# Two transformer blocks on one core: gate products two ahead, VectorE alone around the norms, residual scaled beside the short convolutions, four tiles of the last gate side by side

## Chip, core and metric

The kernel runs on one core of a Trainium2 chip. Its engines work side by side, each through its own queue in program order: TensorE (PE: matmuls and transposes into PSUM banks), VectorE (DVE), ScalarE (ACT), GpSimd (POOL), and SyncE (SP), which issues the transfers. The metric is the device time of one launch in microseconds; the time of a kernel is the median of several runs.

## What is computed

A sequence of 512 positions with 1024 features goes through two blocks (f32, batch 1). The change touches the end of the first block and the second one:

```python
# end of block 1
x = x + merged @ w_out
h = rmsnorm(x, norm_ffn_g)
u = causal_dwconv(h @ w_up, conv_ffn_w)                  # 3 taps
x = x + (silu(gate_f) * up_f) @ w_down                   # d_ff 2816
x = rmsnorm(x, norm_final_g)
...
# block 2
h = rmsnorm_2(x, norm_pre)
xbc, dt_raw, z_ssd, sc_h, sc_b, sc_c, z_sc = split(h @ w_in)
xbc = silu(causal_dwconv_2(xbc, ssd_conv_w, ssd_conv_b))
y_ssd = ssd_chunked(xs, softplus(dt_raw + dt_bias), -exp(a_log), bm, cm, d_skip)
y_ssd = rmsnorm_2(y_ssd * silu(z_ssd), ssd_norm)         # in two groups of 512 features
y_sc = sc_b * causal_dwconv_2(sc_c * sc_h, sc_conv_w) * silu(z_sc)
mix = concat([y_ssd, y_sc]) @ w_out
x = x + rmsnorm_2(mix, norm_post)
return x + sigmoid(x @ w_ple_gate) * (p @ w_ple_proj)
```

## The kernel before

**Tiles and products.** Activations lie feature-major, as tiles of 128 features by 512 positions; 1024 features are 8 tiles. Each f32 operand of a product is split in a rounded part `hi` and the rest `lo = x - hi`, and a product is three matmuls for each pair of tiles: w-hi with x-hi, w-hi with x-lo, w-lo with x-hi. One output tile of a product over 1024 features is thus 24 matmuls into one PSUM bank; four banks (`mm`) serve the products, four (`pt`) the transposes and small products. `linear` makes one output tile; `linears` makes several side by side: for each feature tile the three matmuls of every output tile, then the next feature tile.

**Weights** come as 228 chunks of eight 128x128 blocks, in the order that `order()` writes down. `t_chunk` turns a chunk `raw` into `hi` on ScalarE and `lo` on VectorE or GpSimd. `Emit.idle` makes this choice, and also the one for the normalised tiles `xn` (in `normalised`) and for one addition in `t_x2`: it keeps a model clock of each engine while the program is written out, and gives the instruction to GpSimd if that would be free soon enough, unless VectorE's model clock runs far ahead.

**The order on each engine** is written out once, before the launch. The main line (`block1`, `ffn`, `block2`) asks for products; beside it small tasks (`t_...`) are spawned for evictions, norms and gates. `drive` always advances the task whose operands will be ready first by the model clocks; what has been issued stands in its engine's queue in that order.

**The places of the change.** At the FFN norm (products `out`, then the gate and up products `fg`, `fu`) and at block 2's entry (down products `fd`, then `sh`, `sc` for three tiles, the small product for `dt`, then `xbc`), the products that come first take unnormalised tiles and are scaled behind the product. `unfold` is where the main line goes over to normalised tiles `xn`. At block 2's entry `t_final` computes the two nested norms, has the eight `xn` made, then broadcasts the column `r1` over the partitions (four transposes, one copy, tile `rs1`) and scales the eight residual tiles `xr`, which are used again only in `t_x2` at the end.

In the middle of block 2, for each of eight tiles m: the gate product `zs` (its eviction is a silu), then `short_conv(m)` with the products `sh`, `sc` (from m = 3 on), `sb`, `sz`. `t_ssd(m)` is spawned behind `zs(m)`: it loads four rows, `row` and `Ce`, per pair of heads, makes decay tiles with VectorE, an exp on ScalarE and GpSimd, and runs 28 small matmuls. Two `t_ssd` are in work at most. `t_group(g)` takes the mean square of four finished tiles, broadcasts its inverse root (`rsg`), scales the four tiles and has them split. `mix` is the product over the 16 tiles of both halves: the first eight are y_ssd, the second eight the short convolutions. Then follow `pp` (the projection of p), and with `t_post` the norm of `mix` (its mean square, tile `rspost`); `t_x2` scales `mix`, adds `xr` and splits the sum, which `pg`, the last gate product, reads. The first three tiles of `pg` are made side by side.

Of the kernel before, what the change touches and what calls it, by code (L numbers as in the profile page):

```python
# [13 lines left out]
ALU = mybir.AluOpType  # L14
# [23 lines left out]
PAIR_FFN = 3  # L38
FOLD_FFN = 3
FOLD_B2 = 3  # L40
XBC = [8, 9, 0, 1, 2, 3, 4, 5, 6, 7]


# [60 lines left out]
def order():  # L104


    one = lambda keys: [[k] for k in keys]
    kq = lambda h: one([("k", h), ("q", h)])
    vg = lambda h: one([("v", h), ("ga", h)])
    o = [START] + one([("ckv", 0), ("ckv", 1)]) + [FIRST] + one([("q", 1), ("k", 2), ("q", 2)])  # L110
    for item in GDN_ORDER:
        if item[0] == "kq":
            o += kq(item[1])
        elif item[0] == "vg":
            o += vg(item[1])
        elif item[0] == "low":
            pass
        elif item[0] == "wv":
            o += one([("wv", kt, h) for kt in range(2) for h in range(4 * item[1], 4 * item[1] + 4)])
        elif item[0] in ("bra", "brb", "ya"):  # L120
            o.append([item])
        else:
            h = item[1]
            o += one(qr_of(h) + [("kn", h), ("qn", h)])
    o += [[("yb", 0), ("yb", 1)]] + one([("yb", m) for m in range(2, 8)])
    o += one([("out", m) for m in range(8)])
    pair = lambda f: [("fg", f), ("fu", f)]
    for f in range(12):
        o += [pair(f)] if f < PAIR_FFN else one(pair(f))
    o += one([("fd", 0, m) for m in range(8)])  # L130
    o += one([x for f in range(12, 22) for x in pair(f)])
    o += one([("fd", 1, m) for m in range(8)])
    xbc = [("xbc", m) for m in XBC]
    o += [[("sh", m), ("sc", m)] for m in range(FOLD_B2)] + [["dt2"]] + one(xbc)
    for m in range(8):
        o += one([("zs", m)] + ([("sh", m), ("sc", m)] if m >= FOLD_B2 else []) + [("sb", m), ("sz", m)])
    o += one([("mix", m) for m in range(8)])
    o += one([("pp", m) for m in range(8)])
    o += [[("pg", 0), ("pg", 1), ("pg", 2)]] + one([("pg", m) for m in range(3, 8)])
    return o  # L140


# [252 lines left out]
class Emit:  # L395
# [5 lines left out]
    def __init__(self, ctx, tc, a, out):  # L401
        self.tc, self.a, self.out = tc, a, out
        self.nc = self.tl = Timeline(tc.nc)
        E = ctx.enter_context
        self.const = E(tc.tile_pool(name="const", bufs=1))
        self.wp = E(tc.tile_pool(name="wp", bufs=1))
        self.gp = E(tc.tile_pool(name="gp", bufs=1))
        self.sm = E(tc.tile_pool(name="sm", bufs=1))
        self.ps = E(tc.tile_pool(name="ps", bufs=1, space=PSUM))
        self.dr = E(tc.tile_pool(name="dr", bufs=1, space=DRAM))  # L410
        self.n = 0
        self.nmm = 0
        self.mms = []
        self.held = None
        self.specs = weight_specs()
        self.order = order()
        self.opos = 0
        self.bpos = 0
        self.blocks = {}
        self.his = {}  # L420
        self.nchunk = a["wstream"].shape[0]
        self.loaded = 0
        self.tasks = []
        self.waiting = {}
        self.nspawn = 0
        self.flags = set()
        self.live = []
        self.hold = 1 << 30
        self.using = None

    def idle(self, pool, dve, bias=0):

        now = self.tl.clk["PE"]
        t = lambda e: max(self.tl.clk[e], now)
        if t("DVE") - now > BACKLOG:
            return self.nc.vector
        return self.nc.gpsimd if t("POOL") + pool <= t("DVE") + dve + bias else self.nc.vector
# [918 lines left out]
    def block1(self):  # L1356
        nc = self.nc
# [82 lines left out]
        ps = yield from self.linears(START, self.xh)  # L1440
# [3 lines left out]
        for m in range(2):  # L1444
            ps = yield from self.linear(("ckv", m), self.xh)
            self.spawn(self.t_rows(raws["ckv"], m, ps, None, "lr"))
        yield from self.unfold()
        ps = yield from self.linears(FIRST, self.xh)
# [4 lines left out]
        ps = yield from self.linear(("q", 1), self.xh)  # L1453
# [3 lines left out]
        for item in GDN_ORDER:  # L1457
# [12 lines left out]
            elif item[0] in ("bra", "brb"):  # L1470
                ps = yield from self.linear(item, self.xh)
# [4 lines left out]
            else:  # L1476
# [6 lines left out]
                ps = yield from self.linear(item, oa)  # L1483
# [18 lines left out]
        for ms in [(0, 1)] + [(m,) for m in range(2, 8)]:  # L1502
# [3 lines left out]
            ps = yield from self.linears([("yb", m) for m in ms], ob)  # L1506
# [13 lines left out]
        for m in range(8):  # L1520
            x = self.g(name="xr")
            nc.sync.dma_start(x, self.a["xT"][m])
            ps = yield from self.linear(("out", m), mg)
            self.spawn(t_out(m, x, ps))

    def unfold(self):

        self.hold = self.bpos
        yield lambda: hasattr(self, "xn")
        self.hold = 1 << 30  # L1530
        self.xh = self.xn
        self.fold = None
        del self.xn


    def ffn(self):
        nc = self.nc
        hs = [None] * MFF
        self.fold = True

        def t_gate(d, f, ps, fold):
            d["g"] = yield from self.conv(ps, fold, "conv_ffn_w", f, 3, "fg")
            nc.scalar.activation(d["g"], d["g"], AF.Silu)

        def t_up(d, f, ps, fold):
            up = yield from self.conv(ps, fold, "conv_ffn_w", MFF + f, 3, "fu")
            yield lambda: "g" in d
            yield [d["g"]]
            nc.gpsimd.tensor_tensor(up, d["g"], up, ALU.mult)
            hs[f] = yield from self.split(up)  # L1550

        def pair(f):
            d = {}
            keys = ("fg", f), ("fu", f)
            if f < PAIR_FFN:
                pg, pu = yield from self.linears(keys, self.xh)
                self.spawn(t_gate(d, f, pg, self.fold))
            else:
                pg = yield from self.linear(keys[0], self.xh)
                self.spawn(t_gate(d, f, pg, self.fold))  # L1560
                pu = yield from self.linear(keys[1], self.xh)
            self.spawn(t_up(d, f, pu, self.fold))

        def t_down(half, m, ps):
            yield [ps]
            nc.vector.tensor_tensor(self.xr[m], self.xr[m], ps, ALU.add)
            if half:
                yield from self.final_tile(m)

        def down(half):  # L1570
            for m in range(8):
                ps = yield from self.linear(("fd", half, m), hs[11 * half:11 * half + 11] if not half else hs2)
                self.spawn(t_down(half, m, ps))

        for f in range(12):
            if f == FOLD_FFN:
                yield from self.unfold()
            yield from pair(f)
        yield lambda: hs[10] is not None
        yield from down(0)  # L1580
        for f in range(12, 22):
            yield from pair(f)
        yield lambda: hs[21] is not None
        hs2 = hs[11:]
        self.xh = [None] * 8
        del self.rs
        self.spawn(self.t_final())
        yield from down(1)
        del hs, hs2

# [6 lines left out]
    def t_final(self):  # L1597
        nc = self.nc
# [9 lines left out]
        r1 = yield from self.meanrs(self.x1, D, "fn1")  # L1608
# [10 lines left out]
        nc.gpsimd.tensor_tensor(self.rs2, self.rs, self.rs, ALU.mult)  # L1619
        self.xn = [None] * 8  # L1620
        yield from self.normalised(self.x1, self.gg, self.rs, True, self.xn)
        r1b = yield from self.bcast(r1, "rs1")
        self.xr = self.x1
        for m in range(8):
            nc.vector.scalar_tensor_tensor(self.xr[m], self.xr[m], self.par("norm_final_g", m), r1b,
                                           ALU.mult, ALU.mult)
            yield [self.xr[m]]


    def dts(self):  # L1630

# [258 lines left out]
    def block2(self):  # L1890
        nc = self.nc
# [16 lines left out]
        self.spawn(self.t_group(0))  # L1908
        self.spawn(self.t_group(1))
        zd = {}  # L1910
        for m in range(8):
            ps = yield from self.linear(("zs", m), self.xh)
            self.spawn(self.t_rows(zd, m, ps, AF.Silu, "zs"))
            self.spawn(self.t_ssd(m, zd), "ssd")
            yield from self.short_conv(m)
        mix = [None] * 8
        self.spawn(self.t_post(mix))
        for m in range(8):
            ps = yield from self.linear(("mix", m), self.ym)
            self.spawn(self.t_rows(mix, m, ps, None, "mix"))  # L1920
        ph, pp = [None] * 2, {}
# [4 lines left out]
        for m in range(8):  # L1926
            ps = yield from self.linear(("pp", m), ph)
            self.spawn(self.t_rows(pp, m, ps, None, "pp"))
        x2 = [None] * 8
# [20 lines left out]

        for m in range(8):
            self.spawn(t_x2(m))
        ps = yield from self.linears([("pg", m) for m in range(3)], x2)
        for m in range(3):
            self.spawn(t_fin(m, ps[m]))
        for m in range(3, 7):
            ps = yield from self.linear(("pg", m), x2)
            self.spawn(t_fin(m, ps))

# [69 lines left out]
```

## Time and profile before

| | |
|---|---|
| median of 3 runs | 1471.09 us (1470.6 to 1472.59) |
| profiled execution, its own time | 1473.28 us |
| its span, first to last instruction | 1471.5 us |
| mean granted TensorE clock | 0.993 of full |
| busy: PE, DVE, ACT, POOL | 1444.7, 854.4, 657.8, 542.6 us |

The profile is of one execution. An engine's busy time is the sum of its instructions' durations; matmuls overlap one another, so that a row of a matmul is longer than the time to the next one's start. The granted clock is the share of full speed that the chip's throttle let TensorE have. In a row of the timeline, the bracket gives how long the engine had been idle before the instruction, and which engine's instruction, on which tile, ended that wait.

### The profile page before, as it was taken

Reading aid. Unit: us, or ns where it says so; the run is one execution under the profiler, and the core shown is the slowest. Engines: PE = TensorE matmul, PEld = TensorE weight load, DVE = VectorE, ACT = ScalarE, POOL = GpSimd, SP = SyncE. Lnnn points to the kernel's source line nnn. Section 1 sums busy time; section 2 is a strip of 40 time slices with the busy share of each in tenths; the row PEclk is TensorE's granted clock in tenths of the full one; section 3 lists DMA queues with packets and bytes.
Section 4 is the critical chain, followed back from the end, with each engine's and each line's share of the span. In section 5 each row is a group of like instructions: output and inputs, shape, how many; then the busy total and the mean of one; then the engine's idle time right before and its main releaser. Section 6 shows DMA issues by size and latency. Waiting matters only on the chain.

```text
span 1471.5 us, 18957 instructions
## 1 busy us (share of the span) xinstructions
PE 1444.7 (98%) x7084; PEld 1188.1 (81%) x7084; DVE 854.4 (58%) x1701; ACT 657.8 (45%) x1120; POOL 542.6 (37%) x333
## 2 busy tenths in 40 slices
PE   9999999999999999999999999999999999999998
PEld 6788788778878888888888888888787778878877
DVE  7988879687755554367441244446975564360073
ACT  4664335234555663445442244444544544442342
POOL 0333500520334314434554455444024434534421
PEclk9999999999999999999999999999999999999999
DMA  5434313331122224423333223332233433422322
GB/s 190 134 116 143 108 58 85 117 99 32 58 86 74 85 79 129 150 86 101 100 100 101 90 96 100 100 91 88 67 115 113 117 108 102 135 87 86 100 87 100
DMA packets 56891, 147.62 MB, mean 100 GB/s; under 512 B 15008, under 2 KB 15584, under 8 KB 56800
## 3 DMA queue, kind: packets, MB, share of 16 engines
q1 hardware_dynamic: 56800, 146.42, 32.5%
q8 instruction: 55, 0.90, 0.2%
q14 instruction: 36, 0.29, 0.1%
HBM read 139.48 MB, written 5.34 MB: 98 GB/s over the span
## 4 chain that ended last, share of the span: by engine, by line
PE 79%; DVE 13%; POOL 3%; issue 2%; ACT 1%; DMA 1%; SPq 1%; DVEq 0%; POOLq 0%; ACTq 0%
PE mm L244 71%; PE pt L244 8%; DVE lo L244 3%; POOL st L244 1%; POOL sx L244 1%; DVE st L244 1%; DVE sx L244 1%; DVE mix L244 1%; SPq L244 1%; ACT hi L244 0%; DVE Y L244 0%; DVE rq_u L244 0%; DVE qrs L244 0%; DMA x<-xT 0%; DVE v L244 0%
## 5 line engine op out<-in xcount | busy, mean ns | idle before, releaser
L244 PE MATMUL mm<-hi,hi 128*128 128x512 f32 (+2 forms) x1872 | 741.6, 396 | 3.4 <-ACT hi L244 3.4
L244 PE MATMUL mm<-lo,hi 128*128 128x512 f32 (+2 forms) x1872 | 727.0, 388 | 4.5 <-DVE lo L244 4.5
L244 PE MATMUL mm<-hi,lo 128*128 128x512 f32 (+2 forms) x1872 | 726.7, 389 | 2.5 <-DVE lo L244 2.5
L244 POOL TENSOR_TENSOR lo<-raw,hi 128x1024 fp32r<-128x1024 f32 x152 | 365.2, 2403 | 536.4 <-ACT hi L244 509.0
L244 PEld LDWEIGHTS mm<-hi,lo 128*128 128x128 f32 x1872 | 352.6, 188 | 77.9 <-DVE lo L244 4.2
L244 PEld LDWEIGHTS mm<-hi,hi 128*128 128x128 f32 x1872 | 352.9, 188 | 73.8 <-ACT hi L244 4.3
L244 PEld LDWEIGHTS mm<-lo,hi 128*128 128x128 f32 x1872 | 353.3, 189 | 71.4 <-DVE lo L244 5.6
L244 ACT ACTIVATE hi<-raw 128x1024 fp32r<-128x1024 f32 (+1 forms) x230 | 242.5, 1054 | 229.1 <-PE mm L244 164.4
L244 DVE TENSOR_TENSOR lo<-raw,hi 128x1024 fp32r<-128x1024 f32 (+1 forms) x78 | 97.4, 1249 | 3.5 <-ACT hi L244 3.5
L244 DVE TENSOR_TENSOR sq<-sq,sq 128x512 f32<-128x512 f32 x43 | 32.6, 771 | 93.8 <-ACT sq L244 93.6
L244 DVE TENSOR_TENSOR xr<-xr,mm 128x512 f32<-128x512 f32 x24 | 16.5, 687 | 97.5 <-PE mm L244 97.5
L244 DVE TENSOR_TENSOR lo<-fu,hi 128x512 fp32r<-128x512 f32 x22 | 44.5, 2023 | 42.0 <-ACT hi L244 42.0
L244 DVE SCALAR_TENSOR_TENSOR fu<-mm,params,fu 128x510 f32<-128x510 f32 (+1 forms) x38 | 28.5, 749 | 61.6 <-ACT fu L244 60.9
L244 ACT ACT_TABLE_LOAD x39 | 50.0, 1283 | 13.2 <-DVE k L244 6.0
L244 POOL TENSOR_TENSOR q<-q,row 128x512 f32<-128x512 f32 x8 | 10.6, 1319 | 96.6 <-PE pt L244 86.8
L244 POOL TENSOR_TENSOR fu<-fg,fu 128x512 f32<-128x512 f32 x22 | 30.0, 1365 | 42.8 <-DVE fu L244 42.8
L244 DVE TENSOR_TENSOR lo<-scz,hi 128x512 fp32r<-128x512 f32 x8 | 15.8, 1969 | 32.7 <-ACT hi L244 32.7
L244 POOL TENSOR_TENSOR st<-sl,sx 64x247 f32<-64x247 f32 (+15 forms) x31 | 20.8, 672 | 34.3 <-DVE sx L244 25.0
L244 ACT ACTIVATE fg<-fg 128x512 f32<-128x512 f32 x22 | 13.9, 631 | 40.2 <-DVE fg L244 40.2
L244 DVE SCALAR_TENSOR_TENSOR fg<-mm,params,fg 128x510 f32<-128x510 f32 (+1 forms) x38 | 28.2, 743 | 6.2 <-ACT fg L244 5.5
L244 POOL TENSOR_TENSOR xdd<-xd,dd 128x512 f32<-128x512 f32 x8 | 9.4, 1176 | 60.3 <-DVE xd L244 60.2
L244 DVE TENSOR_TENSOR lo<-pt,hi 128x512 fp32r<-128x512 f32 (+3 forms) x32 | 15.6, 487 | 25.9 <-ACT hi L244 25.7
(312 smaller groups left out, 1552.7 us busy)
## 6 DMA issues: line engine op xcount, KB each, us to landing
raw<-wstream SPq DMA_DIRECT2D x228, 512.0 KB, 3.6
row<-grow_d SPq DMA_DIRECT2D x16, 256.0 KB, 4.4
row<-crow_d SPq DMA_DIRECT2D x16, 256.0 KB, 4.7
x<-xT SPq DMA_DIRECT2D x8, 256.0 KB, 5.9
sbd<-gate SPq DMA_DIRECT2D x8, 256.0 KB, 2.1
sb<-sbd SPq DMA_DIRECT2D x8, 256.0 KB, 3.9
xr<-xT SPq DMA_DIRECT2D x8, 256.0 KB, 3.8
Ce<-crow_d SPq DMA_DIRECT2D x16, 128.0 KB, 5.0
```

What stands on the lines that cost most here:

```text
L244: return f(*args, **kw)
```

## The change

Four things. `PAIR_PG`: the first four tiles of `pg` are made side by side, where three were. `ZS = 2`: the gate products `zs` run two tiles ahead of the short convolutions, and `t_ssd` with them. `norming`: while this flag is set, `idle` gives everything to VectorE; it is set from the seventh `out` product to the FFN's `unfold`, from the seventh `fd` product of the second half to block 2's `unfold`, and from the seventh `mix` product to the end. Residual: the broadcast of `r1` and the eight scalings of `xr` move from `t_final` to a task `t_residual(m)` behind each `short_conv(m)`. The number of instructions on PE, ACT and SP stays what it was; 21 go from POOL (338 to 317) to VectorE (1547 to 1568).

```diff
+PAIR_PG = 4
+ZS = 2
 # order(): the weights' order follows the products
+    o += one([("zs", m) for m in range(ZS)])
     for m in range(8):
-        o += one([("zs", m)] + ([("sh", m), ("sc", m)] if m >= FOLD_B2 else []) + [("sb", m), ("sz", m)])
+        o += one(([("sh", m), ("sc", m)] if m >= FOLD_B2 else []) + [("sb", m), ("sz", m)])
+        if m + ZS < 8:
+            o += one([("zs", m + ZS)])
...
-    o += [[("pg", 0), ("pg", 1), ("pg", 2)]] + one([("pg", m) for m in range(3, 8)])
+    o += [[("pg", m) for m in range(PAIR_PG)]] + one([("pg", m) for m in range(PAIR_PG, 8)])
...
     def idle(self, pool, dve, bias=0):
+        if self.norming:
+            return self.nc.vector
...
         for m in range(8):                                   # block 1, "out"
...
+            self.norming = m >= 6
             ps = yield from self.linear(("out", m), mg)
...
     def unfold(self):
...
+        self.norming = False
...
             for m in range(8):                               # down(half)
+                self.norming = half == 1 and m >= 6
                 ps = yield from self.linear(("fd", half, m), ...)
...
     def t_final(self):
...
-        r1b = yield from self.bcast(r1, "rs1")
         self.xr = self.x1
-        for m in range(8):
-            nc.vector.scalar_tensor_tensor(self.xr[m], self.xr[m], self.par("norm_final_g", m), r1b,
-                                           ALU.mult, ALU.mult)
-            yield [self.xr[m]]
+        self.r1 = r1
+
+    def t_residual(self, m):
+        if m == 0:
+            self.r1b = yield from self.bcast(self.r1, "rs1")
+        yield lambda: hasattr(self, "r1b")
+        yield [self.r1b]
+        self.nc.vector.scalar_tensor_tensor(self.xr[m], self.xr[m], self.par("norm_final_g", m), self.r1b,
+                                            ALU.mult, ALU.mult)
...
-        for m in range(8):                                   # block 2
+        def zs(m):
             ps = yield from self.linear(("zs", m), self.xh)
             self.spawn(self.t_rows(zd, m, ps, AF.Silu, "zs"))
             self.spawn(self.t_ssd(m, zd), "ssd")
+        for m in range(ZS):
+            yield from zs(m)
+        for m in range(8):
             yield from self.short_conv(m)
+            self.spawn(self.t_residual(m))
+            if m + ZS < 8:
+                yield from zs(m + ZS)
...
         for m in range(8):
+            self.norming = m >= 6
             ps = yield from self.linear(("mix", m), self.ym)
```

**Block 2's entry, VectorE.** The rows around the eviction `dtz` of the small product for `dt`: `dtw` is its weights, `sh` and `ysc` belong to the short convolutions, `lo<-raw,hi` is half of a weight chunk. Before:

```order
L244 SCALAR_TENSOR_TENSOR lo_9311<-xn_9273,gg_8547,hi_9302 128x512
L244 SCALAR_TENSOR_TENSOR xr_6104<-xr_6104,params,rs_9299 128x512
L244 TENSOR_TENSOR lo_9322<-raw_9308,hi_9317 128x1024
L244 SCALAR_TENSOR_TENSOR xr_6143<-xr_6143,params,rs_9299 128x512
L244 SCALAR_TENSOR_TENSOR xr_6183<-xr_6183,params,rs_9299 128x512
L244 SCALAR_TENSOR_TENSOR xr_6224<-xr_6224,params,rs_9299 128x512
L244 SCALAR_TENSOR_TENSOR ysc_9352<-sh_9282,params,ysc_9352 128x510
L244 SCALAR_TENSOR_TENSOR ysc_9352<-sh_9282,params,ysc_9352 128x511
L244 SCALAR_TENSOR_TENSOR xr_6265<-xr_6265,params,rs_9299 128x512
L244 COPY dtz_9348<-pt_9331 32x512
```

The same place in the changed kernel:

```order
L249 SCALAR_TENSOR_TENSOR lo_9273<-xn_9252,gg_8547,hi_9268 128x512
L249 TENSOR_TENSOR lo_9280<-raw_9266,hi_9275 128x1024
L249 COPY dtw_9290<-hi_9177 128x4x16
L249 COPY dtw_9290<-lo_9189 128x4x16
L249 COPY dtw_9291<-hi_9177 128x4x16
L249 COPY dtw_9291<-lo_9189 128x4x16
L249 TENSOR_TENSOR sh_9288<-mm_9199,sh_9288 128x512
L249 SCALAR_TENSOR_TENSOR ysc_9325<-sh_9288,params,ysc_9325 128x510
L249 SCALAR_TENSOR_TENSOR ysc_9325<-sh_9288,params,ysc_9325 128x511
L249 COPY dtz_9323<-pt_9306 32x512
```

The five scalings of `xr` that stood between the last `lo` of an `xn` and `dtz` are gone from there, and three more behind it; further up, between the norm's last step and `dtz`, VectorE has all eight `xn`, of which POOL had three, and four weight halves as before; a fifth weight half stands inside the norm's own steps.

**Ahead of `mix`, TensorE.** `pt<-sqc,rs` are the four transposes that broadcast the second group's inverse root; the tile `mm_11469` is `mix`'s first output. Before:

```order
L244 MATMUL mm_11420<-lo_9300,hi_11329 128x512
L244 MATMUL mm_11420<-hi_9277,lo_11331 128x512
L244 MATMUL pt_11458<-sqc,rs_11395 128x128 x4
L244 MATMUL mm_11420<-hi_9302,hi_11329 128x512
L244 MATMUL mm_11420<-lo_9311,hi_11329 128x512
L244 MATMUL mm_11420<-hi_9302,lo_11331 128x512
L244 MATMUL mm_11469<-hi_10574,hi_11329 128x512
```

In the changed kernel the same transposes stand here:

```order
L249 MATMUL mm_11279<-hi_9256,hi_11188 128x512
L249 MATMUL mm_11279<-lo_9261,hi_11188 128x512
L249 MATMUL mm_11279<-hi_9256,lo_11190 128x512
L249 MATMUL pt_11317<-sqc,rs_11254 128x128 x4
L249 MATMUL mm_11279<-hi_9268,hi_11188 128x512
L249 MATMUL mm_11279<-lo_9273,hi_11188 128x512
```

Three matmuls stood between these transposes and `mix`'s first matmul; now there are 99: the end of one product tile and the four products of the last short convolution.

**Ahead of `pg`, VectorE.** From the last step of the inverse root of `mix` to the first tiles that `pg` reads. Before:

```order
L244 SCALAR_TENSOR_TENSOR rs_12071<-rq_u_12073,rs_12071 128x4
L244 SCALAR_TENSOR_TENSOR mix_11556<-mix_11556,params,rspost_12133 128x512
L244 SCALAR_TENSOR_TENSOR mix_11621<-mix_11621,params,rspost_12133 128x512
L244 SCALAR_TENSOR_TENSOR mix_11687<-mix_11687,params,rspost_12133 128x512
L244 TENSOR_TENSOR mix_11556<-mix_11556,xr_6104 128x512
L244 TENSOR_TENSOR mix_11621<-mix_11621,xr_6143 128x512
L244 TENSOR_TENSOR mix_11687<-mix_11687,xr_6183 128x512
L244 TENSOR_TENSOR lo_12170<-mix_11556,hi_12166 128x512
```

In the changed kernel:

```order
L249 SCALAR_TENSOR_TENSOR rs_12071<-rq_u_12073,rs_12071 128x4
L249 TENSOR_TENSOR lo_12140<-raw_12124,hi_12126 128x1024
L249 SCALAR_TENSOR_TENSOR mix_11556<-mix_11556,params,rspost_12120 128x512
L249 TENSOR_TENSOR mix_11556<-mix_11556,xr_6104 128x512
L249 SCALAR_TENSOR_TENSOR mix_11621<-mix_11621,params,rspost_12120 128x512
L249 SCALAR_TENSOR_TENSOR mix_11687<-mix_11687,params,rspost_12120 128x512
L249 TENSOR_TENSOR lo_12167<-mix_11556,hi_12160 128x512
L249 SCALAR_TENSOR_TENSOR mix_11753<-mix_11753,params,rspost_12120 128x512
L249 TENSOR_TENSOR mix_11621<-mix_11621,xr_6143 128x512
L249 TENSOR_TENSOR mix_11687<-mix_11687,xr_6183 128x512
L249 TENSOR_TENSOR mix_11753<-mix_11753,xr_6224 128x512
L249 TENSOR_TENSOR lo_12191<-mix_11621,hi_12184 128x512
```

A weight half now stands ahead of the first `mix`, the first sum follows its scaling at once, and a fourth tile is made before the second tile's `lo`. On ScalarE the `hi` of that same weight chunk stands directly ahead of the copy of `rspost`.

## Rows read from the trace of the kernel before

**Rows 1.** The page, part 1: busy time, share, instructions.

```profile
PE 1444.7 (98%) x7084; PEld 1188.1 (81%) x7084; DVE 854.4 (58%) x1701; ACT 657.8 (45%) x1120; POOL 542.6 (37%) x333
```

**Rows 2.** Groups of instructions: count | busy us, mean ns of one | idle before.

```profile
L244 PE MATMUL mm<-hi,lo 128*128 128x512 f32 (+2 forms) x1872 | 726.7, 389 | 2.5 <-DVE lo L244 2.5
L244 POOL TENSOR_TENSOR lo<-raw,hi 128x1024 fp32r<-128x1024 f32 x152 | 365.2, 2403 | 536.4 <-ACT hi L244 509.0
L244 DVE TENSOR_TENSOR lo<-raw,hi 128x1024 fp32r<-128x1024 f32 (+1 forms) x78 | 97.4, 1249 | 3.5 <-ACT hi L244 3.5
```

**Rows 3.** Windows: length, busy PE PEld DVE ACT POOL, granted clock, DMA share, GB/s.

```profile
650.00:675.00 25.00, 25.00 (x112) 20.72 (x111) 24.40 (x30) 14.53 (x21) 4.32 (x3) 1.00 0.26 82
1025.00:1050.00 25.00, 22.62 (x97) 16.69 (x96) 24.79 (x37) 11.28 (x16) 3.59 (x3) 0.93 0.21 66
```

**Rows 4.** TensorE at block 2's entry: timeline, and the window behind the wait.

```profile
1044.22 0.43 PE L244 MATMUL pt<-sqc,dtz 32*128 32x32 f32 x4 [2.27 <-DVE dtz L244]
...
1045.38:1048.80 3.42, 3.42 (x10) 2.67 (x9) 3.35 (x6) 1.63 (x2) 0.00 (x0) 0.50 0.00 0
```

**Rows 5.** POOL's and VectorE's timelines at block 2's entry.

```profile
1014.83 1.29 POOL L244 TENSOR_TENSOR xn<-xr,rs 128x512 f32<-128x512 f32 x1
...
1016.91 1.01 DVE L244 SCALAR_TENSOR_TENSOR lo<-xn,gg,hi 128x512 fp32r<-128x512 f32 x1 [6.71 <-ACT hi L244]
...
1039.41 2.07 DVE L244 SCALAR_TENSOR_TENSOR xr<-xr,params,rs 128x512 f32<-128x512 f32 x3
```

**Rows 6.** Timeline ahead of mix (PE, VectorE), and the window behind the wait.

```profile
1303.51 0.60 PE L244 MATMUL pt<-sqc,sq 128*128 128x128 f32 x4
...
1304.88 0.17 DVE L244 TENSOR_SCALAR ms_a<-cs 128x4 f32<-128x4 f32 x1
...
1312.84 0.60 PE L244 MATMUL pt<-sqc,rs 128*128 128x128 f32 x4
...
1320.71 0.50 PE L244 MATMUL mm<-lo,hi 128*128 128x512 f32 x1 [3.59 <-DVE lo L244]
...
1322.07:1325.06 2.99, 2.99 (x9) 2.34 (x8) 0.99 (x2) 0.00 (x0) 0.00 (x0) 0.50 0.31 114
```

**Rows 7.** Timeline ahead of pg: VectorE, POOL, ScalarE, TensorE.

```profile
1410.21 2.41 POOL L244 TENSOR_TENSOR lo<-raw,hi 128x1024 fp32r<-128x1024 f32 x1 [3.73 <-ACT hi L244]
...
1410.43 2.20 DVE L244 SCALAR_TENSOR_TENSOR ms_a<-cs,ms_a 128x4 f32<-128x4 f32 x1
...
1414.65 0.16 DVE L244 SCALAR_TENSOR_TENSOR rs<-rq_u,rs 128x4 f32<-128x4 f32 x1
1415.01 1.06 ACT L244 ACTIVATE hi<-raw 128x1024 fp32r<-128x1024 f32 x1
...
1417.06 3.36 DVE L244 SCALAR_TENSOR_TENSOR mix<-mix,params,rspost 128x512 f32<-128x512 f32 x3 [2.25 <-ACT rspost L244]
...
1421.06 1.83 ACT L244 ACTIVATE hi<-mix 128x512 fp32r<-128x512 f32 x3 [1.40 <-DVE mix L244]
...
1421.74 0.49 PE L244 MATMUL mm<-hi,hi 128*128 128x512 f32 x1 [2.70 <-ACT hi L244]
1422.89 0.50 PE L244 MATMUL mm<-lo,hi 128*128 128x512 f32 x1 [0.65 <-DVE lo L244]
...
1429.62 0.50 PE L244 MATMUL mm<-lo,hi 128*128 128x512 f32 x1 [0.28 <-DVE lo L244]
```

**Rows 8.** Timeline at the first SSD products (PE, VectorE, ScalarE), and ScalarE before the second.

```profile
1115.41 2.76 DVE L244 TENSOR_SCALAR row<-row,cmp 128x128 f32<-128x128 f32 x8
...
1117.42 0.64 ACT L244 ACTIVATE row<-row 128x512 f32<-128x512 f32 x1 [5.60 <-DVE row L244]
...
1121.65 0.66 PE L244 MATMUL pt<-row,xd 128*64 128x128 f32 x8
...
1132.79 1.28 ACT L244 ACT_TABLE_LOAD   x1
1134.08 1.20 ACT L244 ACTIVATE row<-row 128x512 f32<-128x512 f32 x2
```

More of the change, by code (lines that the diff above doesn't have):

```diff
@@ L1532, in unfold @@
         self.fold = None
+        self.norming = False
         del self.xn
@@ L1621, in t_final @@
         yield from self.normalised(self.x1, self.gg, self.rs, True, self.xn)
-        r1b = yield from self.bcast(r1, "rs1")
         self.xr = self.x1
-        for m in range(8):
-            nc.vector.scalar_tensor_tensor(self.xr[m], self.xr[m], self.par("norm_final_g", m), r1b,
-                                           ALU.mult, ALU.mult)
-            yield [self.xr[m]]
+        self.r1 = r1
[6 more added lines that the diff above has]
+                                            ALU.mult, ALU.mult)
+        if m == 7:
+            del self.r1b
     def dts(self):
@@ L1952, in block2 @@
             self.spawn(t_x2(m))
-        ps = yield from self.linears([("pg", m) for m in range(3)], x2)
-        for m in range(3):
+        ps = yield from self.linears([("pg", m) for m in range(PAIR_PG)], x2)
+        for m in range(PAIR_PG):
             self.spawn(t_fin(m, ps[m]))
-        for m in range(3, 7):
+        for m in range(PAIR_PG, 7):
             ps = yield from self.linear(("pg", m), x2)
```

## Prediction

> **What bounds the kernel.** I read the page first: TensorE is busy 98% of the span, every other engine under 60% [rows 1]. So only time in which TensorE waits, or runs slower than it can, is to be had. Then I went through the windows of 25 us: nearly all read like the first of [rows 3], TensorE 25.00 of 25 us with 112 matmuls, one for each 0.22 to 0.23 us; I use 0.23. From the FFN norm on, where the change begins, three places are different, and there I read the timelines.
>
> *A, block 2's entry* [rows 4]. The transposes of `dtz` come after 2.27 us of idle, released by VectorE's `dtz`. A matmul row lasts 0.39 us [rows 2] but the next one starts after 0.23, so an idle time of t costs t + 0.16: here 2.43. Soon behind it the granted clock reads 0.50, the 1.2 GHz level, for 3.42 us, in which every matmul takes twice its time: 1.7 lost. A costs 4.1 us. Why `dtz` is late is in the VectorE rows: 24.79 of 25 us busy [rows 3], with eight scalings of `xr` in its queue, five of them directly ahead of `dtz`, 2.07 us for three [rows 5]. Earlier VectorE had been idle for 6.71 us until 1016.91, because the first `xn` was made on POOL at 1014.83, behind a weight half of 2.40 us.
>
> *B, ahead of `mix`* [rows 6]. Group 1's mean square is transposed at 1303.51, its inverse root broadcast at 1312.84; then the scalings, `hi`, `lo`, and TensorE goes on at 1320.71 after 3.59 us of idle: 3.75 lost, and half of the 2.99 us at clock 0.50 behind it, 1.5. B costs 5.25.
>
> *C, ahead of `pg`* [rows 7]. Idle 2.70, 0.65 and 0.28: with 0.16 each 2.86, 0.81 and 0.44, together 4.1. The clock does not fall here.
>
> The ceiling is A + B + C = 13.45 us. Time on VectorE or POOL elsewhere is worth nothing.
>
> **The change part by part.**
>
> *Residual later, and `norming` at block 2's entry (A).* Off VectorE's queue ahead of `dtz` go five `xr`, 0.69 each [rows 5], 3.45 us; on it come three `xn` that POOL made. I have no row of an `xn` on VectorE here; a tile of this size is 0.69 in these rows, so 2.07. More is won at the start: the first `xn` no longer waits for POOL. VectorE was through with the norm at 1010.2 (1016.91 - 6.71); four transposes (0.60, as in [rows 6]) and a copy (0.61, as a `hi` in [rows 7]) put the broadcast at 1011.4, and the first `xn` follows it, not at 1014.83. From there to the last `dtw` the changed order has 21 tile operations, four weight halves and the four small casts: 21 x 0.69 + 4 x 1.2 + 0.4 = 19.7, so 1031.1. TensorE has 93 matmuls between the norm's transposes and the small product, 21.4 us, and wants `dtw` at about 1031.9. Just in time. Behind the small product only six matmuls, 1.4 us, stand ahead of `dtz`'s transposes (fifteen before), with an eviction of 0.7 to be done in them; and the norm's own transposes come six matmuls earlier, while the inserted weight half keeps the root from coming earlier: up to 0.5 of wait. I keep 0.6 us for such small waits. With the long wait the slow stretch should go; the clock is low in these rows only behind the longest idle times (2.27 and 3.59), not behind C's 2.70, so that is not certain. Gain 3.5. Bounds: 1.8 (the wait goes, but the clock falls all the same and the small waits stay) to 4.1.
>
> The moved scalings then stand one behind each short convolution, 0.69 of VectorE per tile of three to five products, 5.5 us each. The broadcast's four transposes move with them and cost TensorE what they did, 0.60 like those of [rows 6]. Nothing.
>
> *`zs` two ahead (B).* Three matmuls stood between group 1's broadcast and `mix`; now 99, 22.8 us. Its mean square's transposes stand 39 matmuls ahead of the broadcast's, 9.0 us, where the rows have 9.3 without a wait. From the broadcast to TensorE's restart took 1320.71 - 1312.84 = 7.9 us, of which twelve `mix` matmuls were covered before as well. All of the wait goes, with 15 us to spare, whatever the added `xr` scaling and weight half there cost (0.7 and 1.2). Gain 5.25; bounds 3.75 (the clock falls at `mix` for another reason) to 5.25.
>
> The price stands at the first SSD products [rows 8]. Tiles 0 and 1 are now prepared together: sixteen VectorE operations where eight take 2.76 us, and ScalarE's order becomes exp, table load, silu of `zs1`, table load, exp, weight `hi`, exp, exp. From the first exp at 1117.42: 0.64, 1.28, 0.60, 1.28, 0.64 gives 1121.9, one product with `cb` on VectorE (0.69) gives 1122.6. TensorE has nine matmuls more to do before it (39, not 30), so it comes at 1121.65 + 2.1 = 1123.7. The second tile: 1121.9 + 1.06 + two exps + 0.69 = 1124.9, needed 28 small matmuls later (0.66 for eight), at about 1126.0. Margin 1.1 in both; cost 0, and at worst rival 2.
>
> *`norming` and four tiles (C).* `ms_a` took 2.20 us, to 1412.63, as long as POOL's weight half beside it (to 1412.62), where 0.17 is usual [rows 6, 7]. POOL does none of these now: 2.0 us won, but one weight half (1.14 to 1.25 [rows 2]) stands inside the norm's steps: the root is ready at about 1413.8 instead of 1414.81. The scalings of `mix` no longer take 3.36 for three, but 0.69 each. Against that: on ScalarE a weight `hi` now stands ahead of the copy of `rspost`, and it can't be sooner than its transfer, 1415.01 to 1416.07; then the `lo` of that chunk, 1.2, ahead of the first scaling, which starts at 1417.25. Scaling, sum, `hi` (0.69, 0.69, 0.61): 1419.2. TensorE comes free at 1421.74 - 2.86 = 1418.9 as before: wait 0.3 to 0.4. The first tile's `lo` comes behind two more scalings, at 1420.4 to 1420.7, where 1419.5 is wanted: 0.9 to 1.2. With four tiles side by side a step is 12 matmuls, 2.7 us, not 2.0, against 2.0 to 2.6 us of VectorE (scaling, sum, `lo`, and a weight half at each second step); I keep 0.3 for the second step. Left 1.65, gain 4.1 - 1.65 = 2.45. Bounds 1.0 (waits as long as the upper values, and two more) and 3.8.
>
> *FFN norm.* No wait of TensorE now, though VectorE is busy 24.40 of 25 us [rows 3]. It gets four weight halves and two `xn`, some 6 us, and loses what POOL's halves stretched. I take nothing; if its cover is gone, that is 0 to 3 us.
>
> Sum: 3.5 + 5.25 + 2.45 = 11.2 from the profiled execution's own 1473.28: 1462.1. That execution is 2.19 us above the median of the runs, so 1471.09 - 11.2 = **1459.9**.
>
> **The rivals.**
>
> 1. *VectorE stays the bound at A.* For it: the queue is full (24.79 of 25), and `idle` now adds to it. The Trainium skill, page "Perfetto Trace Analysis", section "Optimizing Scalar/DVE Operations", says that some work of a saturated VectorE may well be given to GpSimd, which is the reverse of this edit; it adds that the two share a port, so it might not help. Against: VectorE stood idle 6.71 us while POOL made the first `xn` [rows 5], and an instruction of 0.17 took 2.20 beside a POOL one [rows 7]. If the three `xn` and the inserted weight half (2.07 + 1.25) cost as much as the five scalings saved (3.45), A stays whole: 1459.9 + 3.5 = 1463.4.
>
> 2. *A new wait at the first SSD products.* For it: margins of 1.1 us on a chain of eight ScalarE steps. If each of the two loads held ScalarE for twice its 1.28, the tiles would come 1.5 us late (2.56 less 1.1): with the 0.16, and perhaps a slow stretch of 1.7, 1461.5 to 1463.2. Against: an exp starts at 1134.08 right behind a load of 1.28 at 1132.79 [rows 8], so I go by 1.28. The Trainium skill's page "ScalarE: Activation LUTs", section "What ACT_TABLE_LOAD costs", gives 2.66 us in all per switch, of which 1.28 is the load; by that the two switches would take 2.76 more than I count, and the time would be 1461.7 to 1463.4. This trace doesn't show the rest of it.
>
> 3. *C gives nothing back*, because TensorE now waits for the `hi` and `lo` of the weight chunk ahead of `rspost` instead: 1459.9 + 2.45 = 1462.35.
>
> 4. *Slower.* `t_ssd` prepares in the shade of the products, eight rounds; if the new place of `zs` left each round short, each would wait. Against: the loop is the same behind each `zs`, and TensorE has no wait in these rounds now. It decides from 11.2 / 8 = 1.4 us per round; at 2 us with no clock loss it gives 1475.9.
>
> **How the numbers follow.** The forecast's chain 0.64 (own range 1457.6 to 1462); rival 1 0.10, rival 2 0.12, rival 3 0.07; slower 0.04; no effect, since waits only change places, 0.03. Two runs of one kernel tell 0.2% apart, 2.9 us. All of the first four are faster than 1468.2; for misses of several at once I move 0.04 to the other two: faster 0.89, same 0.06, slower 0.05. The range goes from 1457 (the ceiling 1471.09 - 13.45 = 1457.6, rounded down for the runs' own spread) to 1465 (rival 1 with a further 1.5).
>
> **What would show it.** Right: `dtz` released TensorE without idle, VectorE's first `xn` near 1011.4 in place of POOL's; no idle and clock 1.00 around the first `mix`; `ms_a` 0.17 at C and two or three idle times under 1.2 us each at the first `pg`. Wrong: idle over 1 us ahead of the first two SSD tiles, at the FFN norm or at `dt2`, or a clock of 0.50 anywhere from the FFN on; a POOL weight half still beside the norms. If the time stays over 1465, a wait has opened that stands in no row here.

## The result and the profile after

The changed kernel took 1464.43 us in the median of 8 runs (1461.31 to 1468.91), the kernel before 1473.01 us in 8 runs, three of them those given above: ratio 0.9935, 95% interval 0.9924 to 0.9946, that is 9.6 us less (8.0 to 11.2; the two medians alone differ by 8.6). Forecast were 11.2 us less. The profiled execution took 1465.11 us, with a span of 1463.3 us against 1471.5.

The windows of 25 us are read as in [rows 3]. TensorE's idle time is the length of the window, 25.00, less the number behind it; the granted clock stands behind POOL.

```profile
1000.00:1025.00 25.00, 24.91 (x117) 20.48 (x116) 21.86 (x52) 11.14 (x15) 3.22 (x3) 1.00 0.25 68
1025.00:1050.00 25.00, 23.87 (x109) 18.06 (x108) 21.00 (x45) 10.86 (x15) 5.69 (x3) 1.00 0.26 82
1100.00:1125.00 25.00, 24.34 (x148) 18.82 (x146) 14.35 (x28) 11.73 (x14) 10.54 (x9) 1.00 0.43 106
1300.00:1325.00 25.00, 25.00 (x112) 20.71 (x111) 8.32 (x9) 6.30 (x9) 11.22 (x5) 1.00 0.31 98
1400.00:1425.00 25.00, 23.83 (x107) 18.80 (x106) 19.08 (x39) 13.68 (x22) 0.00 (x0) 1.00 0.29 85
```

Ahead of `mix` (around 1310) nothing is lost, and the clock is 1.00 in all five. What is left are four waits, all that the view of waits lists for TensorE from 560 us to the end; here they stand in the timeline:

```profile
1034.43 0.39 PE L249 MATMUL pt<-hi,dtw 128*32 128x512 f32 x1 [1.13 <-DVE dtw L249]
...
1123.27 0.44 PE L249 MATMUL pt<-row,xd 128*64 128x128 f32 x4 [0.66 <-DVE row L249]
...
1413.72 0.49 PE L249 MATMUL mm<-hi,hi 128*128 128x512 f32 x1 [0.39 <-ACT hi L249]
1414.98 0.50 PE L249 MATMUL mm<-lo,hi 128*128 128x512 f32 x1 [0.77 <-DVE lo L249]
```

To these come 0.25 us lost ahead of the norm's transposes at 1011.58 and 0.17 at 1418.05, where the starts lie 0.48 and 0.40 apart and not 0.23. With 0.16 for each idle time over 0.3, as in the prediction, the losses are: entry 0.25 + 1.29, ahead of `pg` 0.55 + 0.93 + 0.17. The first SSD products are small matmuls with shorter distances, and their wait of 0.66 costs 1.1: from the first of them to the next product they take 5.93 us, and 4.85 in a kernel further down in which the same 56 matmuls don't wait (`Ce` of the second tile on VectorE). Together 4.3, where the prediction counted 13.45 before: 9.2 won, inside the interval of the runs.

The span fell by only 8.2. In this execution the granted clock was 0.50, the 1.2 GHz level, from 417.76 on, in a part of the program that the change does not touch: TensorE's matmuls are 0.1 us later than in the profile before ahead of it, and 1.7 behind it, the same up to 990. From there to the end 9.9 us are won, of which the count above finds 9.2. The window before, then after:

```profile
417.76:421.17 3.41, 3.41 (x18) 2.84 (x17) 2.48 (x7) 1.20 (x4) 0.00 (x0) 1.00 0.45 144
...
417.76:421.17 3.41, 3.41 (x11) 2.83 (x11) 1.89 (x5) 0.67 (x2) 0.00 (x0) 0.50 0.44 144
```

At the entry VectorE makes the first `xn`, as forecast, but it is stretched. VectorE and POOL, first piece of the stage:

```profile
1012.86 2.14 DVE L249 TENSOR_TENSOR xn<-xr,rs 128x512 f32<-128x512 f32 x2 [1.42 <-ACT rs L249]
1014.92 2.31 DVE L249 TENSOR_TENSOR lo<-raw,hi 128x1024 fp32r<-128x1024 f32 x1
...
1025.38 1.78 DVE L249 SCALAR_TENSOR_TENSOR lo<-xn,gg,hi 128x512 fp32r<-128x512 f32 x1
...
1033.99 0.19 DVE L249 CAST dtw<-hi 128x64 fp32r<-128x64 f32 x1
...
1012.90 1.55 POOL L249 TENSOR_TENSOR rs<-rs 128x512 f32<-128x512 f32 x1 [30.88 <-ACT rs L249]
1014.52 1.62 POOL L249 TENSOR_TENSOR sh<-sh,rs 128x512 f32<-128x512 f32 x1
1024.95 1.67 POOL L249 TENSOR_TENSOR sh<-sh,rs 128x512 f32<-128x512 f32 x1 [8.80 <-DVE sh L249]
```

`norming` takes from POOL only what `idle` decides. Two kinds of instruction that the code gives to POOL by name are left there: `rs2` and the products of `sh` with it. Each of the three shown lies over a VectorE instruction that is 0.85 to 1.1 us longer than usual. From the start of the first `xn` to the end of the last `dtw` 21.6 us pass, where the prediction had 19.7.

At the first SSD products, VectorE, ScalarE and POOL:

```profile
1113.90 6.42 DVE L249 TENSOR_SCALAR row<-row,cmp 128x128 f32<-128x128 f32 x16
...
1118.00 0.64 ACT L249 ACTIVATE row<-row 128x512 f32<-128x512 f32 x1 [7.70 <-DVE row L249]
1118.65 1.28 ACT L249 ACT_TABLE_LOAD   x1
1119.95 0.60 ACT L249 ACTIVATE zs<-mm 128x512 f32<-128x512 f32 x1
1120.56 1.28 ACT L249 ACT_TABLE_LOAD   x1
1121.86 0.63 ACT L249 ACTIVATE row<-row 128x512 f32<-128x512 f32 x1
...
1112.68 5.01 POOL L249 TENSOR_TENSOR Ce<-Ce,xbc 64x512 f32<-64x512 f32 x4
```

The ScalarE chain from the first exp to the second is what the prediction laid out, load for load (3.86 us against 3.80). But it begins 4.1 us behind the first row operation; before, it was 2.0 [rows 8]. The view of the tile `row` before, with the shortest, median and longest of the eight operations in ns:

```profile
L244 DVE TENSOR_SCALAR row<-row,cmp x8: 273/274/1383, 1115.4 to 1117.9; 128x128 f32<-128x128 f32 x8
```

In the changed kernel three of the sixteen are that long (last section).

### The profile page after: what moved, and what is told of

It reads as the page before. It is cut to its first block, busy times and chain, and to the rows that moved or that the text cites. A ratio compares the mean times of both kernels' runs of the same rounds, so it can differ in the third digit from the quotient of the medians.

```text
span 1463.3 us, 18957 instructions
## 1 busy us (share of the span) xinstructions
PE 1443.4 (99%) x7084; PEld 1187.8 (81%) x7084; DVE 867.9 (59%) x1722; ACT 656.2 (45%) x1120; POOL 497.5 (34%) x312
## 4 chain that ended last, share of the span: by engine, by line
PE 81%; DVE 11%; POOL 3%; issue 2%; ACT 1%; DMA 1%; SPq 1%; DVEq 0%; POOLq 0%; ACTq 0%
PE mm L249 72%; PE pt L249 8%; DVE lo L249 2%; POOL st L249 1%; POOL sx L249 1%; DVE st L249 1%; SPq L249 1%; DVE row L249 1%; DVE sx L249 1%; ACT hi L249 0%; DVE Y L249 0%; DVE qrs L249 0%; DMA sl<-ldram 0%; DVE v L249 0%; DMA x<-xT 0%
## 5 line engine op out<-in xcount | busy, mean ns | idle before, releaser
L249 POOL TENSOR_TENSOR lo<-raw,hi 128x1024 fp32r<-128x1024 f32 x136 | 327.6, 2409 | 462.2 <-ACT hi L249 399.6
L249 DVE TENSOR_TENSOR lo<-raw,hi 128x1024 fp32r<-128x1024 f32 (+1 forms) x94 | 117.1, 1245 | 27.9 <-ACT hi L249 27.9
L249 DVE SCALAR_TENSOR_TENSOR xbc<-mm,params,xbc 128x509 f32<-128x509 f32 (+2 forms) x30 | 22.5, 749 | 9.5 <-ACT xbc L249 8.8
```

The source lines that it names most:

```text
L249: return f(*args, **kw)
```

## Experiments

Ratios are to the kernel before, run beside each kernel; the changed kernel has 0.9935. Losses of TensorE are read from the profiles as above, the changed kernel's being 4.3 us.

**The gate products back in their place.**

```diff
-        for m in range(ZS):
-            yield from zs(m)
         for m in range(8):
+            yield from zs(m)
             yield from self.short_conv(m)
             self.spawn(self.t_residual(m))
-            if m + ZS < 8:
-                yield from zs(m + ZS)
```

(with the weights' order to match.) Expected:

> The changed kernel with the gate products in their old place again (zs(m), then short_conv(m)); the other three parts stay. My account: the order ahead of mix is the old one, so TensorE waits 3.5 us or more there again and the slow stretch of 1.5 may come back (4 to 5.3 us lost at mix), while the 0.7 us at the first SSD products goes: 3.5 to 4.5 us slower than the changed kernel, ratio to the kernel before about 0.996 to 0.997. Rival: the wait at mix went because VectorE and POOL are freer, whatever the order: no idle time at mix, ratio 0.993.

Measured: ratio 0.9969 (0.9954 to 0.9983), 5.0 us above the changed kernel. TensorE's timeline, the window behind the wait, and the first SSD products:

```profile
1320.92 0.80 PE L246 MATMUL mm<-lo,hi 128*128 128x512 f32 x1 [3.59 <-DVE lo L246]
...
1320.92:1324.00 3.08, 3.08 (x8) 2.48 (x9) 2.36 (x4) 0.00 (x0) 0.00 (x0) 0.53 0.64 176
...
1121.39 0.66 PE L246 MATMUL pt<-row,xd 128*64 128x128 f32 x8
```

The wait of [rows 6] is back to the hundredth, and the slow stretch with it; the wait at the first SSD products is gone, all eight run through. B's gain, and that wait, come with the new place of `zs` and go with it.

**Without `norming`.**

```diff
     def idle(self, pool, dve, bias=0):
-        if self.norming:
-            return self.nc.vector
```

> The changed kernel with the flag that gives everything to VectorE taken out; order of products, residual and four tiles stay. My account: ahead of pg the step ms_a is stretched to about 2 us again beside a POOL weight half and the wait is 3 to 4 us again, not 1.75; at block 2's entry the first xn comes from POOL about 3 us later, so dtw or dtz is waited for by 2 us or more. In all 2.5 to 4 us slower than the changed kernel, ratio 0.995 to 0.996. Rival: VectorE alone is what costs at the entry (the wait of 1.3 us for dtw), so that the entry gets faster without it and the ratio stays at 0.993 to 0.994.

Measured: ratio 0.9966 (0.995 to 0.9981), 4.6 us above the changed kernel. Timeline of POOL, VectorE and TensorE ahead of `pg`, a window behind it, and TensorE's two waits at the entry:

```profile
1406.54 2.40 POOL L249 TENSOR_TENSOR lo<-raw,hi 128x1024 fp32r<-128x1024 f32 x1 [3.72 <-ACT hi L249]
...
1406.77 2.19 DVE L249 SCALAR_TENSOR_TENSOR ms_a<-cs,ms_a 128x4 f32<-128x4 f32 x1
...
1418.08 0.51 PE L249 MATMUL mm<-hi,hi 128*128 128x512 f32 x1 [2.70 <-ACT hi L249]
1419.22 0.50 PE L249 MATMUL mm<-lo,hi 128*128 128x512 f32 x1 [0.64 <-DVE lo L249]
...
1420.02:1423.43 3.41, 3.41 (x10) 2.63 (x9) 3.41 (x6) 1.49 (x2) 0.00 (x0) 0.50 0.00 0
...
1038.65 0.50 PE L249 MATMUL mm<-lo,hi 128*128 128x512 f32 x1 [1.16 <-DVE lo L249]
...
1045.13 0.24 PE L249 MATMUL pt<-sqc,dtz 32*128 32x32 f32 x1 [0.65 <-DVE dtz L249]
```

`ms_a` is long again and C's waits are those of [rows 7], 2.70 and 0.64; this time a slow stretch follows, 3.41 us at 0.50, which costs 1.7 and takes the whole above the 2.5 to 4 us expected. At the entry 1.32 + 0.81 are lost, against 1.54 with the flag. So at the entry the flag is worth 0.6 us only.

**The residual back at the entry.**

```diff
+        r1b = yield from self.bcast(r1, "rs1")
         self.xr = self.x1
-        self.r1 = r1
+        for m in range(8):
+            nc.vector.scalar_tensor_tensor(self.xr[m], self.xr[m], self.par("norm_final_g", m), r1b,
+                                           ALU.mult, ALU.mult)
+            yield [self.xr[m]]
...
-            self.spawn(self.t_residual(m))
```

> The changed kernel with the eight scalings of xr back at block 2's entry. My account: they stand in VectorE's queue between the last xn and dtz, 0.69 each, five to eight of them: the wait for dtz comes back with 2 to 4 us, perhaps with a slow stretch of 1.7; 2 to 5 us slower than the changed kernel, ratio 0.995 to 0.997. Rival: the earlier first xn alone made the room, and the scalings fall behind dtz: ratio 0.993 to 0.994.

Measured: ratio 0.9949 (0.9932 to 0.9966), 2.1 us above the changed kernel, but the intervals overlap: the runs alone don't tell the two apart. The profile has 1.5 more lost. VectorE and TensorE:

```profile
1039.09 3.39 DVE L249 SCALAR_TENSOR_TENSOR xr<-xr,params,rs 128x512 f32<-128x512 f32 x5
1042.40 0.67 DVE L249 COPY dtz<-pt 32x512 f32<-32x512 f32 x1
...
1043.13 0.43 PE L249 MATMUL pt<-sqc,dtz 32*128 32x32 f32 x4 [0.90 <-DVE dtz L249]
```

Five scalings stand ahead of `dtz` again, but the wait is 0.90, not 2.27: `dtz` starts 31.0 us behind the norm's transposes (1042.40 - 1011.42), before it was 32.5 (1043.50 - 1011.00). That for `dtw` is 0.62, not 1.13; a wait of 0.79 for `gg` follows at 1052.03. No slow stretch. Of A's 4.1 us, 2.1 are left with the moved residual alone (the kernel without `norming`), 3.0 with the flag alone (this one) and 1.54 with both: the residual is the larger part.

**Three tiles of `pg` side by side** (`PAIR_PG = 3`).

> The changed kernel with three tiles of pg side by side instead of four. My account: the waits before the first two matmuls of pg stay (0.55 and 1.0 us); a step is 9 matmuls (2.0 us) where VectorE needs 2.0 to 2.6 us for a tile, so there are one to three more waits of 0.2 to 0.6 us: 0.3 to 1.2 us slower than the changed kernel, ratio 0.9937 to 0.9945. Rival: the fourth tile only delays the second tile's lo: with three the waits are shorter, ratio 0.993.

Measured: ratio 0.9945 (0.9927 to 0.9963), 1.5 us above the changed kernel, which the runs alone would not tell from none; the profile has 1.35 more lost. TensorE's timeline:

```profile
1414.51 0.51 PE L249 MATMUL mm<-hi,hi 128*128 128x512 f32 x1 [0.38 <-ACT hi L249]
1415.78 0.50 PE L249 MATMUL mm<-lo,hi 128*128 128x512 f32 x1 [0.76 <-DVE lo L249]
...
1418.85 0.50 PE L249 MATMUL mm<-lo,hi 128*128 128x512 f32 x1 [0.65 <-DVE lo L249]
```

The first two waits are unchanged; the second step, which 9 matmuls don't cover, now waits 0.65, and two later ones cost 0.2 and 0.4. In the profile the fourth tile is worth slightly more than I expected.

The next three kernels were measured in one execution each. Executions of one kernel lie up to 7.6 us apart (the changed one's 1461.31 to 1468.91), so their times decide nothing, and what is read is the waits.

**Two `Ce` of the second tile on VectorE**, to take half of POOL's work from beside the row operations.

```diff
-            yield [Cs[e]]
-            nc.gpsimd.tensor_tensor(Cs[e][r], Cs[e][r], self.C[r], ALU.mult)
+            if m != 1:
+                yield [Cs[e]]
+                nc.gpsimd.tensor_tensor(Cs[e][r], Cs[e][r], self.C[r], ALU.mult)
+        if m == 1:
+            for e in range(2):
+                yield Es + [Cs[e]]
+                nc.vector.tensor_tensor(Cs[e][r], Cs[e][r], self.C[r], ALU.mult)
```

> The changed kernel, with the two Ce products of the second tile's pair of heads (t_ssd(1)) on VectorE, behind its products with cb, instead of on POOL. My account: the wait of 0.7 us at the first SSD products comes from POOL: four Ce instead of two stand beside VectorE's row operations, and three of these take 1.3 us instead of 0.28. With two Ce on POOL one or two row operations are long, the first exp comes 1 to 2 us earlier (now 4.1 us behind the first row operation), and the wait of 0.93 from start to start falls to under 0.35. Rival: the two table loads on ScalarE set the time of the second exp: the row operations get shorter, but the wait stays at 0.6 to 0.9.

Measured in one execution: 1461.89 us (its mean granted clock was 0.998, the changed kernel's profile has 0.994). VectorE and ScalarE, and TensorE's first SSD products:

```profile
1111.48 4.32 DVE L249 TENSOR_SCALAR row<-row,cmp 128x128 f32<-128x128 f32 x16
...
1113.48 0.63 ACT L249 ACTIVATE row<-row 128x512 f32<-128x512 f32 x1 [5.60 <-DVE row L249]
...
1119.76 0.66 PE L249 MATMUL pt<-row,xd 128*64 128x128 f32 x8
```

Sixteen row operations take 4.32 us instead of 6.42, one of them being long and not three; the first exp comes 2.0 us behind the first of them; the eight products run through without a wait. Both table loads are still there. The rival falls.

**POOL quiet at the entry.**

```diff
-        nc.gpsimd.tensor_tensor(self.rs2, self.rs, self.rs, ALU.mult)
+        nc.scalar.activation(self.rs2, self.rs, AF.Square)
...
-                nc.gpsimd.tensor_tensor(d["h"], d["h"], self.rs2, ALU.mult)
+                nc.vector.tensor_tensor(d["h"], d["h"], self.rs2, ALU.mult)
```

> The changed kernel, with what POOL still does at block 2's entry taken from it: rs2 is squared on ScalarE, the three products sh times rs2 are made on VectorE. My account: these POOL instructions stretch VectorE's (two xn take 2.14 us and a weight half 2.31 beside them, 1.3 and 1.22 alone): VectorE gets two more operations of 0.7 ahead of dtw but loses about 3 us of stretching, so dtw comes 1 to 1.7 us earlier, and the wait of 1.5 us from start to start falls to 0.2 to 0.7. Rival: VectorE is simply full there, and more work on it makes dtw 1.3 us later: the wait grows to 2.5 us or more.

Measured in one execution: 1463.08 us. VectorE, and the window with TensorE's busy time:

```profile
1012.17 1.29 DVE L249 TENSOR_TENSOR xn<-xr,rs 128x512 f32<-128x512 f32 x2 [1.42 <-ACT rs L249]
...
1014.59 1.22 DVE L249 TENSOR_TENSOR lo<-raw,hi 128x1024 fp32r<-128x1024 f32 x1
...
1031.54 0.19 DVE L249 CAST dtw<-hi 128x64 fp32r<-128x64 f32 x1
...
1025.00:1050.00 25.00, 25.00 (x115) 19.16 (x114) 20.51 (x46) 11.93 (x16) 2.75 (x1) 1.00 0.26 75
```

VectorE does two more operations ahead of `dtw` and reaches it 19.4 us behind the first `xn`, not 21.1. The wait for `dtw` is gone altogether (25.00 of 25 us busy), better than I expected. VectorE was not too full: it was held up.

**`rspost` on VectorE, and the weight half behind the first tile.**

```diff
+        yield lambda: not self.late           # t_chunk, ahead of lo
         lo = part("lo")
...
         r = yield from self.meanrs(mix, D, apart=True)
-        self.rsp = yield from self.bcast(r, "rspost")
+        self.late = True
+        self.rsp = yield from self.bcast(r, "rspost", True)   # True: the copy on VectorE
...
             x2[m] = yield from self.split(t)
+            self.late = False
```

> The changed kernel, with the copy of rspost on VectorE instead of ScalarE (where a weight hi stands ahead of it), and the weight half that VectorE made ahead of the first scaling of mix held back until the first tile is split. My account: these two are what is left of the wait ahead of pg: the first scaling starts 1.3 to 1.5 us earlier, TensorE's waits of 0.77 and 1.26 from start to start fall to under 0.35 each, 1.3 to 1.6 us in all. Rival: the chain from the mean square on sets it, or the held weight half is missed later: the waits stay or move to the second or third step of pg, with less than 0.5 us won.

Measured in one execution: 1463.38 us. VectorE and TensorE:

```profile
1408.84 0.75 DVE L249 SCALAR_TENSOR_TENSOR mix<-mix,params,rspost 128x512 f32<-128x512 f32 x1
...
1413.03 0.50 PE L249 MATMUL mm<-lo,hi 128*128 128x512 f32 x1 [0.48 <-DVE lo L249]
```

The wait for the first `hi` is gone; that for the first `lo` fell only from 1.26 to 0.98 from start to start, since two more scalings and a sum still stand ahead of it. About 0.7 us won, half of what I expected.

**All three edits together.**

> The three edits together: Ce of the second tile on VectorE, rs2 on ScalarE and sh times rs2 on VectorE at the entry, rspost on VectorE with the weight half held back. My account: of the 4.0 us that TensorE still loses behind 430 us, 2.5 to 3.5 go: ratio to the kernel before 0.991 to 0.992, where the changed kernel has 0.9935. Rival: the waits only change places: 0.993 to 0.994.

Measured: 1461.39 us in the median of 6 runs, ratio 0.9912 (0.9898 to 0.9926): faster than the kernel before, and below the changed kernel's 0.9935, though the two intervals touch. The profile has 1.3 us lost, 0.25 at the norm's transposes and the rest at `pg`: 3.0 less than the changed kernel.

**And `t_x2` on two tiles ahead, not three** (`m < 2 or x2[m - 2] is not None`).

> The three edits together, and t_x2 working on two tiles ahead instead of three, so that the first tile's lo stands one scaling earlier in VectorE's queue. My account: the last wait ahead of pg (0.98 us from start to start, released by that lo) falls by up to 0.66 us and nothing else moves: ratio 0.9905 to 0.9915, 0.3 to 0.6 us below the kernel with the three edits, too little to be told from it by the runs, but seen in the profile. Rival: with less work ahead the later steps of pg wait, and what is won comes back there.

Measured: 1460.66 us, ratio 0.9894 (0.9875 to 0.9912), which is not told apart from the one above. TensorE ahead of `pg`:

```profile
1409.62 0.51 PE L249 MATMUL mm<-lo,hi 128*128 128x512 f32 x1 [0.22 <-DVE lo L249]
...
1415.81 0.50 PE L249 MATMUL mm<-lo,hi 128*128 128x512 f32 x1 [0.22 <-DVE lo L249]
```

The first wait is shorter by 0.25 us, and a later step waits by as much: the rival was right.

## Why the forecast held, and where its terms were off

The direction, the range and the mechanism of B and C held, that of A in the main: 9.6 us against 11.2. The time, 1464.43, is 4.5 above the 1459.9 forecast, inside the range up to 1465 but above the 1462 that the chain alone allowed: 1.9 of it is the kernel before, 1473.01 in 8 runs where the forecast started from 1471.09 in three, and 2.6 is what the medians fell short of 11.2. One of the signs of being wrong that the prediction named did show: over 1 us idle at `dt2`, the small product (1.13 for `dtw`).

*B* was forecast at 5.25 and is 5.25 by the same count: no idle time ahead of `mix`, clock 1.00; undone, it comes back to the hundredth.

*C* was forecast at 2.45, with 1.65 left over; 1.65 is left, at the three places named, the weight half ahead of the first scaling among them. `ms_a` is 0.16. That `norming` is what does it is shown by the kernel without it, whose waits are the old ones.

*A* was forecast at 3.5 and is 2.6 (4.1 less 1.54). The step that was mis-sized is "21 x 0.69 + 4 x 1.2 + 0.4 = 19.7": it used durations of undisturbed instructions, as though the flag had silenced POOL, and 21.6 us passed. Three instructions beside POOL's took 3.0 us more, and some 1.1 of that came back, because the next instruction starts before a row ends (the `xn` of 0.68 at 1019.08, the `ysc` behind it at 1019.68). I had put 0.6 for small waits against what became 1.54. The transposes of `dtz`, the place of the old wait, don't wait, and no slow stretch follows, which was 1.7 of the 4.1. The norm's transposes lost 0.25 of the 0.5 allowed for them.

*The first SSD products* were costed at 0 and cost 1.1. The step was "sixteen VectorE operations where eight take 2.76 us": I took the first exp at its old distance, 2.0 us behind the first row operation. In those 2.76 us one operation of 1.38 was hidden beside seven of 0.28; with twice as many `Ce` on POOL it is three of them, all among the first four, and the first exp waits for just these: 2.1 us later, less the margin of 1.1, is about what was lost. So rival 2 came true in its place, somewhat under its lowest price of 1.6, by another cause than the table loads on which I had put it. The Trainium skill's page "ScalarE: Activation LUTs", section "What ACT_TABLE_LOAD costs", gives 2.66 us in all per switch. That is not borne out here: the silu starts 1.30 us behind the load's start, the second exp likewise.

Rival 1 was half right. `norming` at the entry brings 0.6 us as it stands, because the code leaves POOL work beside it; without that, all of the 1.3 us ahead of `dtw` go, though VectorE gets more to do. So giving POOL some of a full VectorE's work, which the Trainium skill's page "Perfetto Trace Analysis" (section "Optimizing Scalar/DVE Operations") says may make sense, would have been the wrong way here; its remark that it might not help agrees with the runs. The FFN norm, costed at nothing, cost nothing: no wait is left there in either profile, and TensorE is 1.7 us later than in the profile before on both sides of it. The round-by-round waits of rival 4 don't show.

Not explained is the slow stretch. C's idle times of 2.70 and 0.64 were followed by none before and by one without `norming`; B's 3.59 had one both times. TensorE's wait of 1.83 us for `X` at 417.5, the same in both profiles, had none before and one in the changed kernel. So the length of a wait alone does not tell, and the prediction's remark that the clock is low only behind the longest idle times (2.27 and 3.59, not 2.70) doesn't hold even in its own rows. That A's stretch comes in every execution of the kernel before is not shown. The mean granted clock was 0.9918 in the 16 executions of it beside the first four experiments and 0.9948 in the 8 of the changed kernel, which makes, as an estimate, 0.003 x 1470 = 4.4 us of the gain: it is of the order of the 3.2 that the prediction put in for A's and B's stretches, but doesn't show where they lay.

## What to carry to other kernels

A wait that depends on one chain is best covered by moving other products behind the chain's start: `zs` two ahead gave back 5.25 us, as forecast, though 1.1 were lost at its new place. Where an engine is to be alone, look for every instruction that the other one is given by name, not only for those that a planner gives out; and where an instruction group has one long member, count what lies beside it before doubling the group.

## What the hardware showed that I had not expected

VectorE and POOL took turns, one instruction each. The first row operations of the changed kernel and the `Ce` beside them, one by one in the timeline:

```profile
1113.90 1.38 DVE L249 TENSOR_SCALAR row<-row,cmp 128x128 f32<-128x128 f32 x1
...
1115.21 1.32 DVE L249 TENSOR_SCALAR row<-row,cmp 128x128 f32<-128x128 f32 x1
...
1116.45 1.32 DVE L249 TENSOR_SCALAR row<-row,cmp 128x128 f32<-128x128 f32 x1
...
1117.69 0.28 DVE L249 TENSOR_SCALAR row<-row,cmp 128x128 f32<-128x128 f32 x1
...
1113.91 1.29 POOL L249 TENSOR_TENSOR Ce<-Ce,xbc 64x512 f32<-64x512 f32 x1
...
1115.16 1.28 POOL L249 TENSOR_TENSOR Ce<-Ce,xbc 64x512 f32<-64x512 f32 x1
...
1116.41 1.27 POOL L249 TENSOR_TENSOR Ce<-Ce,xbc 64x512 f32<-64x512 f32 x1
```

Each of VectorE's starts within 0.05 us of one of POOL's and ends within 0.1 us of that one's end; the fourth, behind the last `Ce`, takes 0.28.

So three operations of 0.28 took as long as three of POOL's. The Trainium skill's page "SBUF — State Buffer", section "Who interferes with whom", has the rule for it: the two engines share a pair of ports, which one instruction holds to its end. These rows agree with that. In them, back-to-back instructions on POOL let through one of VectorE's at a time, however short.
